# First block's merge: own tile for the sum, gates loaded ahead over blocks, DMA queue in a fixed order, four PSUM banks, squares summed on ScalarE

## The chip, the cores and the metric

The kernel runs on one core of one Trainium2 chip. The metric is the device time of one execution in microseconds; the figure of a kernel is the median of its timed runs. Before the change it is 4016.52 us (three runs, 4011.2 to 4027.01).

## The reference

Two transformer-like blocks on 2048 tokens of 1024 features, all in fp32. The change touches only the end of the first block: two scan results (`o_a`, `o_b`) are normed, gated and projected, mixed by sigmoid gates, projected again, added to the input and layer-normed.

```python
def rms_norm_gated(o, gain, gate):
    o = o * lax.rsqrt(jnp.mean(o * o, axis=-1, keepdims=True) + RMS_EPS) * gain
    return o.reshape(*o.shape[:-2], -1) * jax.nn.silu(gate)

def merge_branches(o_a, o_b, p, a_norm_l, b_norm_l, w_a_out_l, w_b_out_l, w_out_l):
    y_a = rms_norm_gated(o_a, a_norm_l, p['a_gate']) @ w_a_out_l
    y_b = rms_norm_gated(o_b, b_norm_l, p['b_gate']) @ w_b_out_l
    gates = jax.nn.sigmoid(p['merge'].reshape(*p['merge'].shape[:-1], N_BRANCH, D_MODEL))
    return (gates[..., 0, :] * y_a + gates[..., 1, :] * y_b) @ w_out_l
...
        h_lat = layer_norm(DEEPNORM_ALPHA * h_lat + gate_l * sub_lat) * ln_g[l] + ln_b[l]
```

The projections in and the scans come ahead of this; the second block (latent attention and a spatial gating unit) takes `h_lat` as its input.

## The kernel before

Every product of fp32 matrices is three matmuls of a high and a low part (`mm3`, L187 to L189), so each factor has to be split: a cast for the high part on ScalarE (ACT) and a subtraction for the low part on GpSimd (POOL) or VectorE (DVE).

The stage that changes takes the 2048 tokens in eight blocks of 256, in the order 4, 3, 5, 2, 6, 1, 7, 0. A block has three parts:

- `branch`, for each half `j` of 128 tokens: three loads (`d_oa` L1329, `d_ob` L1330, the output gate L1332), SiLU of the gate (L1333), the squares of all eight heads in one ACT instruction (L1335), their sums in one DVE reduction (L1338), the inverse root by small DVE operations (L176 to L184), the scaling (L1340). `turned` then transposes on TensorE (PE) (L1346) and makes `yh`, `yl` (L1351, L1352).
- `merge`, eight steps `m`, one for each 128 output features: load a gate tile `mg` of 128x512 (L1360, three buffers), tanh (L1362), two products `pp` of 12 matmuls each (one for each branch, PSUM tag `pp`, two banks), a multiplication by the gate on DVE after each (L1368), the sum of the two in the place of the first, `mg[:, 0]` (L1370), its high part `mh` on ACT (L1371) and its low part `ml` on POOL (L1372). The buffer of `mg` is thus free when POOL is done.
- `residual`, for each half `j`: load `xt` from the input (L1404, two buffers), 48 products `acc` (six of them for each feature group `k`, which wants `mh` and `ml` of step `k`), scaling and sum (L1412), a layer norm on DVE (L1269 to L1276), the store to `d_h` (L1417). Between the products of the first and the second half PE does the transposes of the next block's branches.

In the last block the branches' place is taken by `ahead_h`: the first weights of the second block are loaded (`raw`, L1303) and split, and rows of `d_h` from earlier blocks are loaded back (L1394) and transposed (`turn`, L1374 on). After the last residual come two more turns, then the second block's first products `d`.

All DMAs of the stage are issued by SyncE (SP), each engine takes its instructions in the order of its own list, and an instruction that waits holds back what stands behind it. PE's order is that of the code (`manual_schedule(engines=PE_ONLY)`); the lists of the other engines, SP's too, are set by a scheduler when the kernel is built. `d_h` is viewed as four rows of the token grid by 32 columns, `xt` and `d_oa` likewise; `d_ob` and the gates have their 128 partitions outermost.

Of the kernel before, what the change touches and what calls it, by code (L numbers as in the profile page):

```python
# [21 lines left out]
P = 128  # L22
D = 1024
KT = 8
# [33 lines left out]
MGB = 3  # L58
# [33 lines left out]
def block_kernel(ctx: ExitStack, tc: tile.TileContext, A, out):  # L92
# [31 lines left out]
    # ---------------------------------------------------------------- constants  # L124
# [6 lines left out]
    def tri(pl, name, base, mult, step, keep=1.0, fill=0.0):  # L131
        """keep where base + mult * partition + step * column >= 0, else fill."""
        t = pl.tile([P, P], F32, name=name)
        pool.memset(t, keep)
        pool.affine_select(out=t, in_=t, pattern=[[step, P]], compare_op=ALU.is_ge, fill=fill, base=base,
                           channel_multiplier=mult)
        return t
# [32 lines left out]
    def rsqrt(pl, v, y, eps, tag, mul=1.0, eng=None):  # L170
        """y = 1 / sqrt(mul * v + eps), by a bit estimate and three Newton steps."""
# [19 lines left out]
    # ---------------------------------------------------------------- u^T: layer norm, modulation  # L191
    # tokens by column of the grid: the first and the second half of the columns, the context
# [64 lines left out]
    def proj_stream(jobs, first=()):  # L257
        """The same for several groups of columns, product by product: yields the time of each."""
# [21 lines left out]
    def ahead_of(groups):  # L280
        """Pieces of several groups of columns, each group's weights loaded before the pieces of the one before."""
# [19 lines left out]
    def rotary(rot, sa, sb, pps):  # L301
        """Rotary tables by token: [cos cos | -sin sin]."""
# [8 lines left out]
        # reduction modulo 2 pi: the quotient in a high and a low part, 2 pi in three  # L311
# [24 lines left out]
    with ExitStack() as s0:  # L336
# [3 lines left out]
        # staging in the place of the second half  # L340
# [33 lines left out]
        with tc.manual_schedule(engines={mybir.EngineType.SP}):  # L374
# [4 lines left out]
            # rows silu(c)^T w_mod of shift and scale, for x and for the context  # L379
# [20 lines left out]
            # and by feature, two blocks of tokens at once  # L400
# [77 lines left out]
        # lower bounds: softmax over the two rows of lb_param, first component  # L478
# [14 lines left out]
        # gate of the residual, silu(c) w + b, as a row: products and sums by partition on VectorE, then over partitions  # L493
# [41 lines left out]
    def interleave(*streams, first=0):  # L535
        """Emit the pieces of several streams evenly mixed; all but the last stream are scheduled ahead of it."""
# [39 lines left out]
    with tc.tile_pool(name="tb", bufs=1, side="right") as tb, tc.tile_pool(name="tbs", bufs=1, space=PSUM) as tbs, \  # L576
# [3 lines left out]
        # 16 columns: the four blocks of 512 tokens side by side in the array  # L580
# [75 lines left out]
        # gate tables of the delta rule  # L656
# [16 lines left out]
        # log1p(e) = 2 atanh(e / (2 + e))  # L673
# [59 lines left out]
    # ---------------------------------------------------------------- delta rule: triangular inverses, attention  # L733
    def pair_mats(h, d, m):
        """Matrices of the pair m of chunks: triangular, attention, scaled queries."""
# [575 lines left out]
    with ExitStack() as mctx:  # L1311
# [111 lines left out]
        for j in range(2):  # L1423
            branch(order[0], j)()
# [628 lines left out]
```

## Time and profile before

| | us |
|---|---|
| median of three runs | 4016.52 |
| profiled execution: its span (no other time of this execution is given) | 4017.7 |
| the changed stage, from the first product of the first block to the last of the last | about 2221 to 2746 |
| first block | 71.5 |
| blocks two to seven, together | 381.2 |
| last block | 72.3 |
| PE busy in the whole span | 3665.3 |
| the first product `d` of the second block | starts at 2758.78 |

A time in the profile is counted from the span's start. A block is taken here to run from the last product `acc` of the block before it to its own last one. A view of waits tells which engine sat idle, and the instruction of another engine, or the DMA, that ended the idle time.

### The profile page before, as it was taken

To read this page: it belongs to the slowest core of one execution; us is meant where nothing else is said; L and a number is where in the kernel's file an instruction comes from. 1 tells how busy PE (TensorE), PEld (TensorE's weight loads), DVE (VectorE), ACT (ScalarE), POOL (GpSimd) and SP (SyncE) were. 2 spreads that over 40 slices of the span, in tenths; PEclk is the share of its full clock that TensorE was granted. 3 is DMA by queue.
4 is the path that set the end of the run, shared out by engine and by line. 5 is a ranking of instruction groups with operands and counts; after the bars stand their busy time and mean duration, and the time that the engine had idled before them with its cause. 6 is when DMAs were issued, how large, how long until landed. Compare 5 with 4: busy or idle time off the path is not lost.

```text
span 4017.7 us, 60424 instructions
## 1 busy us (share of the span) xinstructions
PE 3665.3 (91%) x19974; PEld 2833.5 (71%) x19974; DVE 2421.5 (60%) x6610; ACT 1417.1 (35%) x3703; POOL 1399.3 (35%) x1880
## 2 busy tenths in 40 slices
PE   4799998888999999999889778878999999999999
PEld 0578877777677777777677677777888865555577
DVE  3545658886433333699997746455504377777656
ACT  0544542221133323477665322212212144444400
POOL 2311124431355555354643311111123246666610
PEclk9899999999899999999999889888999999999999
DMA  5322247753354554344444433324433520001254
GB/s 159 110 61 78 87 155 240 222 171 73 112 149 139 151 153 140 109 126 123 132 118 132 145 98 102 103 82 118 128 97 115 171 59 26 26 18 48 63 168 147
DMA packets 515309, 467.44 MB, mean 116 GB/s; under 512 B 87993, under 2 KB 424227, under 8 KB 514804
## 3 DMA queue, kind: packets, MB, share of 16 engines
q1 hardware_dynamic: 514772, 463.53, 38.5%
q8 instruction: 159, 2.61, 0.3%
q14 instruction: 154, 1.26, 0.1%
q0 software_dynamic: 224, 0.05, 0.0%
HBM read 302.08 MB, written 161.37 MB: 115 GB/s over the span
## 4 chain that ended last, share of the span: by engine, by line
PE 32%; DMA 7%; DVE 7%; issue 4%; ACT 1%; SPq 1%; POOL 0%; DVEq 0%; ACTq 0%; POOLq 0%
PE po L1830 3%; PE d L187 3%; PE d L188 3%; PE d L189 3%; DMA d_h<-xt 2%; PE acc L187 2%; PE acc L188 2%; PE acc L189 2%; PE sx L1767 2%; PE st L1797 2%; DMA mg<-d_gate 2%; PE st L1798 1%; PE st L1799 1%; DMA o<-d_ob 1%; DMA raw<-in_w_in_dram 1%
## 5 line engine op out<-in xcount | busy, mean ns | idle before, releaser
L187 PE MATMUL d<-uBh,whi 128*128 128x512 f32 x832 | 363.3, 437 | 17.1 <-ACT gy L835 12.3
L187 PE MATMUL d<-uAh,whi 128*128 128x512 f32 x832 | 361.2, 434 | 8.9 <-DVE gy L845 6.8
L188 PE MATMUL d<-uAl,whi 128*128 128x512 f32 x832 | 336.6, 405 | 6.9 <-DVE uAl L463 6.9
L234 POOL TENSOR_TENSOR wlo<-wraw,whi 128x512 fp32r<-128x512 f32 x128 | 172.8, 1351 | 475.4 <-ACT whi L233 453.4
L188 PE MATMUL d<-uBl,whi 128*128 128x512 f32 x832 | 335.2, 403 | 0.0
L189 PE MATMUL d<-uAh,wlo 128*128 128x512 f32 x832 | 334.0, 402 | 0.0
L189 PE MATMUL d<-uBh,wlo 128*128 128x512 f32 x832 | 332.7, 400 | 0.0
L1803 ACT ACTIVATE pT<-st 128x512 f32<-128x512 f32 (+1 forms) x320 | 170.0, 532 | 234.2 <-PE st L1799 140.5
L1821 POOL TENSOR_TENSOR acc<-acc,pT 128x512 f32<-128x512 f32 (+1 forms) x168 | 186.0, 1107 | 124.8 <-ACT pT L1803 115.0
L1772 DVE TENSOR_REDUCE mx<-sx 128x1 f32<-128x512 f32 (+3 forms) x288 | 169.3, 616 | 50.6 <-PE sx L1767 32.7
L187 PEld LDWEIGHTS d<-uBh,whi 128*128 128x128 f32 x832 | 160.3, 193 | 53.4 <-ACT gy L835 13.1
L1372 POOL TENSOR_TENSOR ml<-mg,mh 128x256 fp32r<-128x256 f32 x64 | 57.7, 903 | 396.9 <-ACT mh L1371 289.0
L187 PEld LDWEIGHTS d<-uAh,whi 128*128 128x128 f32 x832 | 160.9, 193 | 43.5 <-ACT pre L769 5.3
L189 PEld LDWEIGHTS d<-uBh,wlo 128*128 128x128 f32 x832 | 159.8, 192 | 35.7
L189 PEld LDWEIGHTS d<-uAh,wlo 128*128 128x128 f32 x832 | 160.6, 193 | 34.6
L188 PEld LDWEIGHTS d<-uAl,whi 128*128 128x128 f32 x832 | 161.5, 194 | 29.4 <-DVE uAl L463 7.8
L188 PEld LDWEIGHTS d<-uBl,whi 128*128 128x128 f32 x832 | 160.7, 193 | 22.2 <-DVE uBl L463 0.4
L187 PE MATMUL pp<-yh,w_a_out_h 128*128 128x256 f32 x256 | 85.3, 333 | 91.9 <-DVE mg L1368 91.1
L631 DVE SCALAR_TENSOR_TENSOR y<-st,VT,y 128x512 f32<-128x512 f32 (+1 forms) x224 | 164.0, 764 | 4.6
L1830 PE MATMUL po<-pT,v 128*64 128x512 f32 (+3 forms) x640 | 161.3, 563 | 3.3 <-DVE o L1844 3.3
L999 DVE SCALAR_TENSOR_TENSOR r<-pa,c_r,r 128x128 f32<-128x128 f32 x136 | 47.7, 351 | 173.0 <-PE pa L998 169.3
L818 DVE TENSOR_TENSOR Mt<-M 128x1 f32<-128x1 f32 (+40 forms) x155 | 134.8, 870 | 4.0
(596 smaller groups left out, 10585.7 us busy)
## 6 DMA issues: line engine op xcount, KB each, us to landing
wraw<-in_w_in_dram SPq DMA_DIRECT2D x126, 256.0 KB
k<-d_k SPq DMA_DIRECT2D x72, 384.0 KB
d_p<-pre SPq DMA_DIRECT2D x64, 384.0 KB
d_gate<-gy SPq DMA_DIRECT2D x96, 256.0 KB
rows<-d_rows SPq DMA_DIRECT2D x36, 512.0 KB
pr<-d_p SPq DMA_DIRECT2D x64, 256.0 KB
mg<-d_gate SPq DMA_DIRECT2D x64, 256.0 KB
wm<-in_w_mod_dram SPq DMA_DIRECT2D x24, 512.0 KB
```

The costliest lines, as they stand in the source:

```text
L187: pe.matmul(out=out, lhsT=lh, rhs=rh, start=start, stop=False)
L188: pe.matmul(out=out, lhsT=lh, rhs=rl, start=False, stop=False)
L189: pe.matmul(out=out, lhsT=ll, rhs=rh, start=False, stop=stop)
L234: pool.tensor_tensor(out=lo[:, ks, :n], in0=raw[:, :, :n], in1=hi[:, ks, :n].bitcast(F32), op=ALU.subtract)
L631: dve.scalar_tensor_tensor(out=y[:, :w], in0=st[:, o + j:o + j + w], scalar=tap, in1=y[:, :w], op0=ALU.mult, op1=ALU.add)
L818: dve.tensor_tensor(out=t, in0=M[:w, i:i + 1, i + 1:32].to_broadcast([w, L, L]), in1=M[:w, i + 1:32, i + 1:32].rearrange("p j c -> p c j") ...
L1767: pe.matmul(out=ps[:, :w], lhsT=qh[0:96, j * P:(j + 1) * P], rhs=kTh[h % 2][0:96, b * 512:b * 512 + w], start=True, stop=not last)
L1772: dve.tensor_reduce(out=m4[:, j:j + 1] if one else mx[:, j, b:b + 1], in_=ps[:, :w], op=ALU.max, axis=AX.X)
L1797: pe.matmul(out=ps[:, c0:], lhsT=kt_h[0:100, ks], rhs=qh[0:100, c0:], start=True, stop=False)
L1803: act.activation(out=pT[:, c0:], in_=ps[:, c0:], func=AF.Exp, scale=SCALE)
L1821: (dve if on_dve else pool).tensor_tensor(out=acc[:, c0:], in0=src[:, c0:], in1=pT[:, c0:], op=ALU.add)
L1830: pe.matmul(out=po_[h, g][r:r + 64, c0:], lhsT=val[kb][:, vs], rhs=pT_.pop((h, g, kb))[:, c0:], start=kb < 2, stop=kb >= 4 * g + 2, skip_g ...
```

## The change

1. The sum of the two gated products has a tile of its own, `ms` (one buffer); `mh` and `ml` are made from it, and a gate's buffer is free when DVE has added.
2. `MGB` is 4. The gate of step `m + 4`, also of the next block, is loaded after step `m` (`load_gates`, the list `todo`).
3. SP's order is now that of the code (`manual_schedule` for PE and SP): the six branch loads of the next block before the merge, the store of the first half in `residual`, that of the second half in step 1 of the next merge, the loads of `xt` in steps 2 and 5.
4. The products `pp` have a PSUM pool of their own with four banks, which one `turn` uses too.
5. The squares of a head are summed by the ACT instruction that makes them: eight of 128x128 for each half, and no DVE reduction.

```diff
-MGB = 3
+MGB = 4
...
-            sq = br.tile([P, KT, P], F32, tag="sq", name="sq")
-            act.activation(out=sq, in_=o, func=AF.Square)
...
-            dve.tensor_reduce(out=ss, in_=sq, op=ALU.add, axis=AX.X)
+            for k in range(KT):
+                sq = br.tile([P, P], F32, tag="sq", name="sq", bufs=2)
+                act.activation(out=sq, in_=o[:, k, :], func=AF.Square, accum_out=ss[:, k:k + 1])
...
-                    pp = m1s.tile([P, 512], F32, tag="pp", name="pp")[:, 0:256]
+                    pp = m1p.tile([P, 512], F32, tag="pp", name="pp")[:, 0:256]
...
-                dve.tensor_add(mg[:, 0, :], mg[:, 0, :], mg[:, 1, :])
-                act.copy(out=mh[:, m, :], in_=mg[:, 0, :])
-                pool.tensor_tensor(out=ml[:, m, :], in0=mg[:, 0, :], in1=mh[:, m, :].bitcast(F32), op=ALU.subtract)
+                ms = m1.tile([P, 256], F32, tag="ms", name="ms")
+                dve.tensor_add(ms, mg[:, 0, :], mg[:, 1, :])
+                act.copy(out=mh[:, m, :], in_=ms)
+                pool.tensor_tensor(out=ml[:, m, :], in0=ms, in1=mh[:, m, :].bitcast(F32), op=ALU.subtract)
+                for f in also.get(m, ()):
+                    f()
+                if todo:
+                    load_gates(*todo.pop(0))
...
-                sp.dma_start(out=hv[4 * i:4 * i + 4], in_=xt)
+                if j == 0:
+                    store_h(i, xt)
...
+        m1p = mctx.enter_context(tc.tile_pool(name="m1p", bufs=4, space=PSUM))
...
-        mctx.enter_context(tc.manual_schedule(engines=PE_ONLY))
+        mctx.enter_context(tc.manual_schedule(engines={mybir.EngineType.PE, mybir.EngineType.SP}))
+        mgs, xs = [], []
+        todo = [(b, m) for b in order for m in range(KT)]
+        for _ in range(MGB):
+            load_gates(*todo.pop(0))
+        last = None
...
+            also = {1: [], 2: [lambda b=b: load_x(b, 0)], 5: [lambda b=b: load_x(b, 1)]}
+            if last is not None:
+                also[1].append(lambda: store_h(2 * order[n - 1] + 1, last))
+            loaded = [branch_load(order[n + 1], j) for j in range(2)] if n + 1 < len(order) else None
...
+                between = [branch(j, *loaded[j]) for j in range(2)]
...
+            last = done[1][0]
+        store_h(2 * order[-1] + 1, last)
```

**SP, from one block into the next, before.** `o` and `sg` are the branch loads, `mg` the gates, `d_h<-xt` the stores, `xt<-in_x_dram` the loads of the input.

```order
L1332 DMA sg_25829<-d_gate_112 128x8x128
L1329 DMA o_25853<-d_oa_98 128x1x512
L1330 DMA o_25853<-d_ob_99 128x512
L1332 DMA sg_25856<-d_gate_112 128x8x128
L1360 DMA mg_25656<-d_gate_112 128x2x256
L1417 DMA d_h_100<-xt_25362 4x32x1024
L1360 DMA mg_25690<-d_gate_112 128x2x256
L1404 DMA xt_25880<-in_x_dram 128x1x1024
L1360 DMA mg_25724<-d_gate_112 128x2x256
L1360 DMA mg_25758<-d_gate_112 128x2x256
L1417 DMA d_h_100<-xt_25458 4x32x1024
L1360 DMA mg_25792<-d_gate_112 128x2x256
```

The branch loads stand ahead of a block's gates, and each store behind a gate of the next block. The same place now:

```order
L1416 DMA d_h_100<-xt_25220 4x32x1024
L1328 DMA o_25658<-d_oa_98 128x1x512
L1329 DMA o_25658<-d_ob_99 128x512
L1331 DMA sg_25661<-d_gate_112 128x8x128
L1328 DMA o_25663<-d_oa_98 128x1x512
L1329 DMA o_25663<-d_ob_99 128x512
L1331 DMA sg_25666<-d_gate_112 128x8x128
L1361 DMA mg_25701<-d_gate_112 128x2x256
L1416 DMA d_h_100<-xt_25327 4x32x1024
L1361 DMA mg_25737<-d_gate_112 128x2x256
L1412 DMA xt_25772<-in_x_dram 128x1x1024
L1361 DMA mg_25774<-d_gate_112 128x2x256
```

The first half's store now stands ahead of the next branches' loads, and those ahead of the block's first gate (that of step 4); the second half's store stands between the gates of steps 4 and 5.

**ACT, from the last branch of a block into the next merge, before.** `yh` ends a branch; a cast `mh` ends a merge step on ACT.

```order
L1351 CAST yh_24229<-sg_25829 128x4x128 [waits DVE_49] x2
L1335 ACTIVATE sq_26350<-o_26344 128x1024 [waits DMAHW4_49,DMAHW3_49]
L1333 ACTIVATE sg_26347<-sg_26347 128x1024 [waits DMAHW5_49,DVE_49]
L1351 CAST yh_24229<-sg_25856 128x4x128 [waits DVE_49] x2
L1335 ACTIVATE sq_26377<-o_26371 128x1024 [waits DMAHW7_49,DMAHW6_49,Activation_49]
L1333 ACTIVATE sg_26374<-sg_26374 128x1024 [waits DMAHW0_49,DVE_49]
L1371 CAST mh_24418<-mg_26072 128x256 [waits DVE_49,PE_49]
L1371 CAST mh_24418<-mg_26106 128x256 [waits DVE_49,PE_49]
```

Both branches' squares and SiLUs stand ahead of the first cast. The same place now:

```order
L1354 CAST yh_24229<-sg_25666 128x4x128 [waits DVE_49] x2
L1341 ACTIVATE sq_26508,ss_26506<-o_26210 128x128 [waits DMAHW5_49]
L1341 ACTIVATE sq_26510,ss_26506<-o_26210 128x128
L1341 ACTIVATE sq_26512,ss_26506<-o_26210 128x128 [waits Activation_49]
L1341 ACTIVATE sq_26514,ss_26506<-o_26210 128x128 [waits Activation_49]
L1341 ACTIVATE sq_26516,ss_26506<-o_26210 128x128 [waits DMAHW6_49,Activation_49]
L1379 CAST mh_24447<-ms_26249 128x256 [waits DVE_49,PE_49]
L1341 ACTIVATE sq_26518,ss_26506<-o_26210 128x128 [waits Activation_49]
L1341 ACTIVATE sq_26520,ss_26506<-o_26210 128x128 [waits Activation_49]
L1341 ACTIVATE sq_26522,ss_26506<-o_26210 128x128 [waits Activation_49]
L1336 ACTIVATE sg_26213<-sg_26213 128x1024 [waits DMAHW7_49]
L1341 ACTIVATE sq_26543,ss_26541<-o_26215 128x128 [waits DMAHW0_49,Activation_49]
```

Five squares of the next block's first half, which want both of its loads, now stand ahead of the cast of step 0; the rest of the branches is strewn between the casts of steps 0 to 3.

**DVE, in the first steps of a merge, now** (L1375 multiplies by the gate, L1378 adds into `ms`, L1276 ends the layer norm of the block before, whose store follows it).

```order
L1375 SCALAR_TENSOR_TENSOR mg_25916<-mg_25916,pp_26292 128x256 [waits PE_49]
L182 TENSOR_TENSOR ln1rz_26195<-ln1rs_26187 128x1 [waits DVE_49]
L1378 TENSOR_TENSOR ms_26284<-mg_25881 128x256 [waits Pool_49]
L176 TENSOR_SCALAR m1rz_26525<-ss_26506 128x8 [waits Activation_49]
L183 TENSOR_TENSOR ln1rz_26195<-ln1rz_26195,ln1rh_26194 128x1 [waits DVE_49]
L177 TENSOR_SCALAR rs_26507<-m1rz_26525 128x8 [waits DVE_49]
L184 SCALAR_TENSOR_TENSOR ln1rs_26187<-ln1rz_26195,ln1rs_26187 128x1 [waits DVE_49]
L180 TENSOR_SCALAR m1rh_26524<-m1rz_26525 128x8
L178 TENSOR_SCALAR rs_26507<-rs_26507 128x8 [waits DVE_49]
L1276 SCALAR_TENSOR_TENSOR xt_25879<-xt_25879,ln1rs_26187,lnb_24847 128x1024 [waits DVE_49]
L1375 SCALAR_TENSOR_TENSOR mg_25916<-mg_25916,pp_26306 128x256 [waits PE_49]
```

The sum of step 1 waits for POOL (step 0's `ml`), and behind it stand the sums of squares, the end of the layer norm and the second multiplication of step 2. Before, the sum waited for no other engine:

```order
L1370 TENSOR_TENSOR mg_26106<-mg_26106 128x256 [waits DVE_49]
L184 SCALAR_TENSOR_TENSOR rs_26353<-m1rz_26356,rs_26353 128x8 [waits DVE_49]
L178 TENSOR_SCALAR ln1rs_26048<-ln1rs_26048 128x1 [waits DVE_49]
L1340 TENSOR_TENSOR o_26344<-o_26344,rs_26353 128x1024 [waits DMAHW4_49,DMAHW3_49,DVE_49]
L182 TENSOR_TENSOR ln1rz_26056<-ln1rs_26048 128x1 [waits DVE_49]
```

Further on, ACT's list has the tanh of the next block's gates 0 and 1 ahead of this block's casts of steps 5 and 6. On SP, in the last block, all eight loads of the next weights (`raw`, 128x416) now stand ahead of the first loads of `h`; before, two of them did.

## Rows read from the trace of the kernel before

**Rows 1.** Chain of waits, 2100 to 2900 us: shares of the stretch by line.

```profile
by line: issue 17.0%; DMA d_h<-xt 12.4%; DMA mg<-d_gate 8.1%; DMA o<-d_ob 4.3%; PE acc L188 4.3%; PE acc L187 4.3%; PE acc L189 4.1%; DMA raw<-in_w_in_dram 3.6%; PE d L187 2.7%; PE pp L187 2.5%; PE d L188 2.2%; PE d L189 2.2%; PE pp L188 2.
```

**Rows 2.** Windows by block; columns: length, busy time of engines, granted clock, DMA share, GB/s.

```profile
2221.00:2292.50 71.50, 56.08 (x304) 50.18 (x305) 54.12 (x98) 27.97 (x46) 31.08 (x24) 0.85 0.55 160
2292.50:2356.10 63.60, 50.93 (x306) 45.68 (x304) 34.34 (x105) 14.27 (x24) 7.43 (x8) 0.92 0.32 100
...
2611.60:2673.70 62.10, 51.65 (x305) 46.50 (x304) 36.20 (x114) 12.05 (x22) 7.44 (x8) 0.92 0.25 77
2673.70:2746.00 72.30, 54.84 (x321) 49.23 (x319) 29.29 (x73) 14.31 (x30) 14.71 (x17) 0.88 0.36 104
```

**Rows 3.** Groups by line, blocks two to seven: busy, mean ns | idle time before, releaser.

```profile
L187 PE MATMUL pp<-yh,w_a_out_h 128*128 128x256 f32 x192 | 63.3, 329 | 67.1 <-DVE mg L1368 67.1
...
L1372 POOL TENSOR_TENSOR ml<-mg,mh 128x256 fp32r<-128x256 f32 x48 | 44.3, 922 | 343.6 <-ACT mh L1371 264.4 <-issue 49.1 <-PE pp L189 30.1
...
L1362 ACT ACTIVATE mg<-mg 128x512 f32<-128x512 f32 x48 | 30.2, 630 | 198.7 <-DMA mg<-d_gate 197.2 <-POOL ml L1372 1.5
...
L1371 ACT CAST mh<-mg 128x256 fp32r<-128x256 f32 x48 | 19.1, 398 | 33.6 <-DVE rs L184 26.4 <-DVE mg L1370 4.3 <-DVE ln1rs L184 2.8
...
L1276 DVE SCALAR_TENSOR_TENSOR xt<-xt,ln1rs,lnb 128x1024 f32<-128x1024 f32 x13 | 16.6, 1279 | 0.0
...
L1335 ACT ACTIVATE sq<-o 128x1024 f32<-128x1024 f32 x11 | 11.7, 1060 | 25.6 <-DMA o<-d_ob 25.6
```

**Rows 4.** Chain of waits, third and fourth block: start, length, what.

```profile
2366.54 10.06 DMA d_h<-xt
2377.28 10.03 DMA mg<-d_gate
2415.34 5.69 DMA o<-d_ob
2430.55 10.14 DMA d_h<-xt
2441.37 9.30 DMA mg<-d_gate
```

**Rows 5.** Timeline of SP, a merge and the last block: start, time to issue, DMA.

```profile
2440.71 0.57 SPq L1404 DMA_DIRECT2D xt<-in_x_dram  x1
...
2715.02 0.82 SPq L1303 DMA_DIRECT2D raw<-in_w_in_dram  x2
2715.89 2.50 SPq L1394 DMA_DIRECT2D h<-d_h  x4
2719.34 28.02 SPq L1303 DMA_DIRECT2D raw<-in_w_in_dram  x9
```

**Rows 6.** Timeline of ACT: summed squares of an earlier stage; start, length.

```profile
259.29 0.27 ACT L646 ACTIVATE sq<-tr 128x128 f32<-128x128 f32 x1
...
259.53 0.28 ACT L646 ACTIVATE sq<-tr 128x128 f32<-128x128 f32 x1
```

**Rows 7.** Timeline of PE, the last block: start, length modelled, product, idle before.

```profile
2673.51 0.40 PE L189 MATMUL acc<-w_out_h,ml 128*128 128x512 f32 x1
2673.74 0.28 PE L187 MATMUL pp<-yh,w_a_out_h 128*128 128x256 f32 x1
...
2683.69 0.28 PE L189 MATMUL pp<-yh,w_a_out_l 128*128 128x256 f32 x1
...
2695.38 0.58 PE L187 MATMUL pp<-yh,w_a_out_h 128*128 128x256 f32 x1 [9.34 <-DVE mg L1368]
...
2698.96 0.41 PE L188 MATMUL pp<-yl,w_b_out_h 128*128 128x256 f32 x1
```

**Rows 8.** Chain of waits in the last block: one weight piece, then the next.

```profile
2737.90 2.39 DMA raw<-in_w_in_dram
...
2740.93 1.09 POOL lo L1306
2742.03 2.98 DMA raw<-in_w_in_dram
```

More of the change, by code (lines that the diff above doesn't have):

```diff
@@ L1321, in block_kernel, with branch_load @@
         hv = d_h.rearrange("(r w) f -> w r f", w=GW)
-        def branch(b, j):
+        def branch_load(b, j):
             i = 2 * b + j
@@ L1332, in branch @@
             sp.dma_start(out=sg, in_=d_gate[:, 0:8, ts_])
+            return o, sg
+        def branch(j, o, sg):
             act.activation(out=sg, in_=sg, func=AF.Silu)
-            sq = br.tile([P, KT, P], F32, tag="sq", name="sq")
-            act.activation(out=sq, in_=o, func=AF.Square)
             ss = br.tile([P, KT], F32, tag="ss", name="ss", bufs=2)
             rs = br.tile([P, KT], F32, tag="rs", name="rs", bufs=2)
-            dve.tensor_reduce(out=ss, in_=sq, op=ALU.add, axis=AX.X)
+            for k in range(KT):
+                sq = br.tile([P, P], F32, tag="sq", name="sq", bufs=2)
+                act.activation(out=sq, in_=o[:, k, :], func=AF.Square, accum_out=ss[:, k:k + 1])
             rsqrt(br, ss, rs, 1e-6, "m1r", mul=1.0 / P)
@@ L1354, in branch, with load_gates, merge @@
             return turned
-        def merge(b):
+        def load_gates(b, m):
+            mg = m1.tile([P, 2, 256], F32, tag="mg", name="mg", bufs=MGB)
+            sp.dma_start(out=mg, in_=d_gate[:, 8 + m:24:8, b * 256:(b + 1) * 256])
+            mgs.append(mg)
+        def merge(b, also):
             for m in range(KT):
-                bs = slice(b * 256, (b + 1) * 256)
-                mg = m1.tile([P, 2, 256], F32, tag="mg", name="mg", bufs=MGB)
-                sp.dma_start(out=mg, in_=d_gate[:, 8 + m:24:8, bs])
+                mg = mgs.pop(0)
                 act.activation(out=mg, in_=mg, func=AF.Tanh, scale=0.5)
                 for s in range(2):
-                    pp = m1s.tile([P, 512], F32, tag="pp", name="pp")[:, 0:256]
+                    pp = m1p.tile([P, 512], F32, tag="pp", name="pp")[:, 0:256]
                     for k in range(4):
@@ L1377, in turn @@
             for s in range(2):
-                tp = m1s.tile([P, 4, P], F32, tag=tag, name="tp")
+                tp = (m1p if tag == "pp" else m1s).tile([P, 4, P], F32, tag=tag, name="tp")
                 for k in range(4):
@@ L1395, in ahead_h, with load_x, store_h @@
                 turn(t, 8, nw, "(r w)", w0, "tp" if w0 in (16, 8) else "pp")
+        def load_x(b, j):
+            xt = m1.tile([P, D], F32, tag="xt", name="xt", bufs=2)
+            i = 2 * b + j
+            sp.dma_start(out=xt, in_=xv[4 * i:4 * i + 4])
+            xs.append(xt)
+        def store_h(i, xt):
+            sp.dma_start(out=hv[4 * i:4 * i + 4], in_=xt)
         def residual(b, between):
@@ L1402, in residual @@
                 js = slice(j * P, (j + 1) * P)
-                xt = m1.tile([P, D], F32, tag="xt", name="xt", bufs=2)
-                sp.dma_start(out=xt, in_=xv[4 * i:4 * i + 4])
+                xt = xs.pop(0)
                 acc = [m1s.tile([P, 512], F32, tag="acc", name="acc") for s in range(2)]
@@ L1423, in block_kernel @@
         for j in range(2):
-            branch(order[0], j)()
+            branch(j, *branch_load(order[0], j))()
         for _ in left:
@@ L1442, in block_kernel @@
             f()
-        mctx.enter_context(tc.manual_schedule(engines=PE_ONLY))
-        for n, b in enumerate(order):
-            merge(b)
+        mctx.enter_context(tc.manual_schedule(engines={mybir.EngineType.PE, mybir.EngineType.SP}))
[4 more added lines that the diff above has]
+        last = None
+        for n, b in enumerate(order):
+            also = {1: [], 2: [lambda b=b: load_x(b, 0)], 5: [lambda b=b: load_x(b, 1)]}
+            if last is not None:
+                also[1].append(lambda: store_h(2 * order[n - 1] + 1, last))
+            loaded = [branch_load(order[n + 1], j) for j in range(2)] if n + 1 < len(order) else None
+            merge(b, also)
             if n == 0:
@@ L1450, in block_kernel @@
                 lnb = bcast_row(lnp, A["ln_b"][0], D, "lnb")
-            if n + 1 < len(order):
-                between = [branch(order[n + 1], j) for j in range(2)]
+            if loaded:
+                between = [branch(j, *loaded[j]) for j in range(2)]
             else:
```

## The prediction, made before the changed kernel ran

> **What bounds the kernel now.** The windows by block come first [rows 2]. The six middle blocks take 381.2 us, 63.5 each, and PE is busy for about 51.5 of them (first and last of six shown), so some 12 us of each block can be won at most by feeding PE better. The groups by line say where those 12 us lie [rows 3]: the first product of a merge step sat idle for 67.1 us in six blocks, 11.2 a block, released by the DVE multiplication of an earlier step. That is only the nearest link. ACT's tanh was idle for 197.2 us until a gate's DMA landed, and POOL for 264.4 until ACT's cast. So PE waits for a PSUM bank, the bank for DVE, DVE for the tanh, the tanh for a transfer. The chain of waits, read third, names the transfers [rows 1]: 12.4% of 800 us on the stores of `d_h`, 8.1% on gates, 4.3% on `d_ob`.
>
> Why a gate takes so long is in two pairs of rows [rows 4, 5]. A store is issued at 2366.54 and lands 10.06 later; the gate behind it and an `xt` load needs 10.03. A block on, the store needs 10.14, `xt` is issued at 2440.71, and the gate behind that lands 9.30 after its issue at 2441.37. Yet the DMA share of a block is 0.25 to 0.33 [rows 2]. A store or `xt` load (four outer rows) therefore costs ten microseconds of landing time, for itself and for whatever is queued behind it, though most engines are idle. The order of this queue sets the block.
>
> [...]
>
> **Cheap parts.** The tile `ms` and the earlier release of `mg` take POOL's subtraction, 0.92 us, off the gate's reuse [rows 3]; on a queue with ten-microsecond transfers that is nothing. Summing squares on ACT: an earlier stage starts one such 128x128 square every 0.25 us [rows 6], so 8 take 2.0 where one of 1024 took 1.06 [rows 3]; 1.9 us a block more on ACT, which is busy 14 of 64, less on DVE, busy 34 of 64 [rows 2]. By itself nothing; its place in ACT's list is what costs.
>
> **A middle block, rebuilt.** Zero is the block's start, the last product of the block before. A product `pp` takes 0.119 us at full clock (84 from 2673.74 to 2683.69), and `acc` 0.23; after a gap the next 16 steps took 3.58 us, 0.22 each [rows 7], the clock's lower level, so a gap costs about 1.5 more than its length.
>
> First wait. SP's list now has the first half's store at the front, the six branch loads behind it, then gate 4. The store is ready at about 0.2 and lands at 9.9, by 10.06 [rows 4]. `d_oa` is half as many bytes in four rows; between 5.69, the whole landing of a pair today [rows 4], and a quarter of the store's ten, I take 2.8: it lands at 12.7, `d_ob` at 13.4. ACT has five squares ahead of the cast of step 0: cast at 14.1. POOL adds 0.92: 15.3 with the handoffs. On DVE the sum of step 1 waits for that (one `ms`), and behind it stand small operations, the end of the layer norm (1.28) and the second multiplication of step 2: bank free at 17.8. PE meanwhile has the gates of steps 0 to 3 and four banks: nine half steps of 12 products, 9 x 12 x 0.119 = 12.9. It waits 4.9.
>
> Second wait. The layer norm ended on DVE at 17.4, so the second half's store goes out at 17.5 and lands near 29, by 10 to 11. Gate 5 is behind it: 29.9, tanh 0.63, multiplication, bank at 31.0. PE, back at 17.8, has five half steps, 60 products with 16 of them slow: 17.8 + 3.6 + 44 x 0.119 = 26.6, 27.0 with handoffs. It waits 4.0.
>
> Third wait. The load of `xt` for the first half is queued behind that store and lands at 35; the second half's needs the buffer stored at 29 and is issued at 32.5. Behind it stands the next block's gate 1, which lands ten later, 43.2, by the gate's 9.30 and 10.03 [rows 4]. Its tanh stands on ACT ahead of the cast of step 6: cast 44.2, `ml` 45 at the latest. PE is through its products at 35.3 and, after 18 of `acc`, wants `ml` of step 6 at 40; with POOL's part only late by its last piece it goes on at 44.3. It waits 4.3.
>
> From there 78 `acc` products follow, 17.9, with 1.5 for the slow start and about 2 for 16 transposes, 21.4: the block ends at **65.7**. Before it was 63.5. The same kind of sum leaves out handoffs: 51.5 busy and 11.2 of waits give 62.7, 0.8 short. So I take 2.2 + 0.8 = **+3 a block, +18 for six**. The waits themselves are 13.2 against 11.2: the gates do come ahead, but three waits, each behind a four-row transfer, stand where two were. Bounds: if `d_oa` costs nothing behind the store, the first wait is 2.1 and the block 62.9, -0.6; if it costs 5.7 and each gap 2 us more, it is +8.
>
> **First and last block.** The first has no store ahead of its loads and four gates ready; one gate wait less or one more is 8 either way, and I take -2. In the last block the branch loads are gone, so its first wait is too, -5. Against that, the loads of `h` stand behind eight weight loads instead of two. Two buffers turn over every 2742.03 - 2737.90 = 4.13 us for a pair's step [rows 8], about 2 us each, so the six more cost 12.4 before `h` is issued, which today is 0.87 after the first weights [rows 5]. PE's transposes of `h` stand between its `acc` products, in two groups. I take half of the 12.4 as covered by the products ahead of them and the rest as a wait at each group, 6 us twice: +12, an estimate between 0 (all covered) and 20. Sum +7, between 0 and +15. Nothing behind this stage changes place.
>
> **Sum.** 18 - 2 + 7 = +23 us. The profiled span of 4017.7 is 1.2 over the median of 4016.52, so the forecast from the median is **4040 us**.
>
> **Rivals.**
>
> Faster: the gates are really ahead and PE stops waiting for them. Then up to 11.2 a block go, and with half to all of it 34 to 67 less, +5 from the ends: 3957 to 3990, say 3973. For it speaks that gates are issued four steps early and that POOL is out of the loop; against, that the landing times stay and that stores and `xt` now have fixed places ahead of gates. It decides itself by whether the branch loads delay the first cast. [...]
>
> No change: the waits move and the sum stays, 11 to 13 a block. With the +7 of the end and -2 of the start: 4005 to 4028, say 4020. This includes the case that the change doesn't do what it says, because the next block's gates are loaded early but their tanh holds back this block's casts.
>
> Slower by more: one `ms` makes a merge step a chain through three engines, an addition, the cast 0.40, `ml` 0.92 [rows 3] and their handoffs, with squares and SiLU between the casts of steps 0 to 3. A step's 24 products take 2.86 at full clock; if the chain takes over 3.5 in the four steps with branch work, 0.7 x 4 x 8 = 22 more come on top: 4062 to 4090.
>
> **How the numbers follow.** Chances: forecast 0.48 (4021 to 4060), faster 0.19, no change 0.21, slower by more 0.12. A measurement tells about 0.5%, 20 us, from no change: faster means below 3996, slower above 4037. About 0.16 of the forecast's chance lies below 4037, as all of the no-change case does. So faster 0.19, same 0.37, slower 0.44. The range, 3972 to 4066, holds the forecast, no change, and parts of the two others; about 0.1 lies on each side.
>
> **What would show it.** Right: at a block's start the store, then `d_oa`, with ACT's squares idle until about 13 us and PE without a product from 13 to 18; gate 5 landing near 30 behind the second store; a cast of step 6 directly after the tanh of a next gate; PE busy unchanged in a block of 65 to 67. Wrong: merge steps that run through without a gap of 3 us, a store that lands in well under 9 us, or blocks of 57 and less. In the last block, `h` should be issued 12 us or more after the first weights; if PE doesn't wait for it, the +12 is wrong.

## The result, and the profile after

The changed kernel takes 4045.35 us (median of four runs, 4042.35 to 4050.16) against 4015.78 before (four runs, 4011.2 to 4027.01). The ratio is 1.0064, with a 95% interval of 1.0045 to 1.0083: slower by 18 to 33 us. The forecast was 4040. The profiled execution of the changed kernel spans 4040.6 us, 22.9 more than the one before. The medians in the table of the experiments are over all executions of a kernel; one of the ten of e4 took 4098.02 us at a granted clock of 0.87 and is left out of its ratio.

The stretches that answer to [rows 2], first block, blocks two to seven together, last block (columns as there):

```profile
2221.95:2295.87 73.92, 56.91 (x304) 49.19 (x305) 51.89 (x104) 29.00 (x75) 29.50 (x24) 0.82 0.52 150
2295.87:2692.98 397.11, 318.95 (x1825) 283.20 (x1824) 201.25 (x613) 100.61 (x324) 39.16 (x48) 0.89 0.32 96
2692.98:2772.40 79.42, 54.95 (x320) 49.32 (x319) 30.45 (x75) 14.53 (x29) 15.65 (x17) 0.81 0.36 101
```

The six middle blocks take 397.1 us in place of 381.2: 66.2 each against 63.5. That is 15.9 of the 22.9 us. The first block is 2.4 longer. From the last block's start to the first product `d` of the second block it is 88.3 against 85.0 (2692.98 to 2781.29, and 2673.74 to 2758.78), 3.3 more. The rest, 1.3, lies outside these stretches.

The groups by line of blocks two to seven, as in [rows 3], show where the waits went:

```profile
L187 PE MATMUL acc<-w_out_h,mh 128*128 128x512 f32 x192 | 82.2, 428 | 24.6 <-ACT mh L1379 24.6
...
L187 PE MATMUL pp<-yh,w_a_out_h 128*128 128x256 f32 x192 | 59.2, 308 | 15.4 <-DVE mg L1375 15.4
...
L1369 ACT ACTIVATE mg<-mg 128x512 f32<-128x512 f32 x48 | 29.9, 627 | 105.5 <-DMA mg<-d_gate 105.3
L1341 ACT ACTIVATE sq<-o 128x128 f32<-128x128 f32 x96 | 28.5, 298 | 111.0 <-DMA o<-d_oa 111.0
L1378 DVE TENSOR_TENSOR ms<-mg 128x256 f32<-128x256 f32 x48 | 20.3, 422 | 95.2 <-POOL ml L1380 95.2
```

The tanh's wait for gates has fallen from 197.2 to 105.3 us: the gates do come ahead. But the squares now wait 111.0 us for `d_oa`, the sum on DVE waits 95.2 for POOL, which it did not do before, and PE waits 24.6 before `acc`, where the same line of the kernel before (`acc` at L187, blocks two to seven) shows 0.0:

```profile
L187 PE MATMUL acc<-w_out_h,mh 128*128 128x512 f32 x192 | 75.8, 395 | 0.0
```

One block, the fourth, from the product at 2427.33 to that at 2494.69. First its transfers on SP (start, time to issue):

```profile
2427.73 0.55 SPq L1416 DMA_DIRECT2D d_h<-xt  x1
2428.38 0.55 SPq L1328 DMA_DIRECT2D o<-d_oa  x1
...
2445.95 0.54 SPq L1416 DMA_DIRECT2D d_h<-xt  x1
2446.54 0.47 SPq L1361 DMA_DIRECT2D mg<-d_gate  x1
...
2460.78 0.57 SPq L1412 DMA_DIRECT2D xt<-in_x_dram  x1
2465.92 8.79 SPq L1361 DMA_DIRECT2D mg<-d_gate  x3
```

then what ACT makes of them:

```profile
2441.10 0.31 ACT L1341 ACTIVATE sq<-o 128x128 f32<-128x128 f32 x1 [16.30 <-DMA o<-d_oa]
...
2442.58 0.39 ACT L1379 CAST mh<-ms 128x256 fp32r<-128x256 f32 x1
...
2457.98 0.63 ACT L1369 ACTIVATE mg<-mg 128x512 f32<-128x512 f32 x1 [5.29 <-DMA mg<-d_gate]
...
2472.13 0.63 ACT L1369 ACTIVATE mg<-mg 128x512 f32<-128x512 f32 x1 [5.75 <-DMA mg<-d_gate]
2472.67 0.39 ACT L1379 CAST mh<-ms 128x256 fp32r<-128x256 f32 x1
```

DVE's sum of step 1 and the end of the layer norm behind it:

```profile
2443.80 0.43 DVE L1378 TENSOR_TENSOR ms<-mg 128x256 f32<-128x256 f32 x1 [8.36 <-POOL ml L1380]
...
2444.64 1.28 DVE L1276 SCALAR_TENSOR_TENSOR xt<-xt,ln1rs,lnb 128x1024 f32<-128x1024 f32 x1
```

and PE's three waits:

```profile
2446.30 0.58 PE L187 MATMUL pp<-yh,w_b_out_h 128*128 128x256 f32 x1 [5.64 <-DVE mg L1375]
...
2459.12 0.39 PE L187 MATMUL pp<-yh,w_a_out_h 128*128 128x256 f32 x1 [2.33 <-DVE mg L1375]
...
2473.11 0.79 PE L187 MATMUL acc<-w_out_h,mh 128*128 128x512 f32 x1 [4.73 <-ACT mh L1379]
```

The lines form one chain. The store goes out 0.4 us into the block, `d_oa` behind it lands at 13.8, ACT has five squares and then the cast of step 0 at 15.3, POOL lets the sum of step 1 go at 16.5, the layer norm ends, the next store goes out at 18.6 with a gate behind it (tanh at 30.7), and the next block's gate behind the second `xt` (issued at 33.4) has its tanh at 44.8, directly ahead of the cast that `acc` wants. That gate, the first of the three in the last SP line, was issued only at 38.6, when DVE's sum of step 5 had freed its buffer; the chain of waits has it as

```profile
2465.92 6.13 DMA mg<-d_gate
```

### The profile page after: what moved, and what is told of

Same layout as the page of the kernel before. It is cut to its first block, busy times and chain, and to the rows that moved or that the text cites. A ratio compares the mean times of both kernels' runs of the same rounds, so it can differ in the third digit from the quotient of the medians.

```text
span 4040.6 us, 60597 instructions
## 1 busy us (share of the span) xinstructions
PE 3672.8 (91%) x19974; PEld 2837.7 (70%) x19974; DVE 2408.9 (60%) x6594; ACT 1438.0 (36%) x3943; POOL 1392.5 (34%) x1880
## 4 chain that ended last, share of the span: by engine, by line
PE 33%; issue 7%; DVE 6%; DMA 4%; POOL 1%; ACT 1%; SPq 0%; DVEq 0%; POOLq 0%; ACTq 0%
PE d L187 4%; PE d L188 4%; PE d L189 4%; PE po L1863 3%; PE acc L187 2%; PE acc L189 2%; PE acc L188 2%; PE sx L1800 2%; PE st L1830 2%; PE st L1831 1%; PE st L1832 1%; DMA mg<-d_gate 1%; POOL ml L1380 1%; PE ms L187 1%; DMA h<-d_h 1%
## 5 line engine op out<-in xcount | busy, mean ns | idle before, releaser
L187 PE MATMUL d<-uBh,whi 128*128 128x512 f32 x832 | 363.1, 437 | 16.9 <-ACT gy L835 12.5
L187 PE MATMUL d<-uAh,whi 128*128 128x512 f32 x832 | 361.7, 435 | 9.2 <-DVE gy L845 6.7
L187 PEld LDWEIGHTS d<-uBh,whi 128*128 128x128 f32 x832 | 160.3, 193 | 52.9 <-ACT gy L835 13.3
L1380 POOL TENSOR_TENSOR ml<-ms,mh 128x256 fp32r<-128x256 f32 x64 | 51.7, 807 | 416.9 <-ACT mh L1379 416.9
L187 PEld LDWEIGHTS d<-uAh,whi 128*128 128x128 f32 x832 | 160.7, 193 | 43.3 <-ACT pre L769 6.2
L187 PE MATMUL acc<-w_out_h,mh 128*128 128x512 f32 x256 | 109.8, 429 | 31.9 <-ACT mh L1379 31.9
```

Source lines behind the costliest of these rows:

```text
L187: pe.matmul(out=out, lhsT=lh, rhs=rh, start=start, stop=False)
L1380: pool.tensor_tensor(out=ml[:, m, :], in0=ms, in1=mh[:, m, :].bitcast(F32), op=ALU.subtract)
```

## The experiments

The code of `hv`, `xv` and `oav` puts the columns of the token grid outermost, so a whole transfer is four columns of 32 rows; the section on the kernel before has it the other way round. The "four outer rows" are these four columns.

The theory: what costs is the ten microseconds of each transfer with four outer rows, because few of the 16 DMA engines work in it (share 0.27 early in a store's flight) and what is queued behind it lands late (gate 5 above: 11.4 us from its issue at 2446.54 to its tanh); the change moves other work behind such transfers. The rivals: the single tile `ms`, the squares on ACT, the fixed order of SP as such, the loads of `h` in the last block. "Blocks" below is the mean of the six middle blocks, from the first product `pp` of one to that of the next in the trace; each ratio is to runs of the kernel before on the same chip.

| kernel | median us | ratio, 95% interval | blocks us |
|---|---|---|---|
| changed, branch loads late (e1) | 4090.5 | 1.0188, 1.0169 to 1.0207 | 72.5 |
| changed, sum in place (e2) | 4049.4 | 1.0074, 1.0055 to 1.0094 | 67.6 |
| changed, all transfers cut by column (e3) | 3893.9 | 0.9690, 0.9676 to 0.9705 | 46.7 |
| before, all transfers cut by column (e5) | 3914.5 | 0.9739, 0.9724 to 0.9753 | 52.1 |
| changed, h first (e4) | 4026.9 | 1.0014, 1.0002 to 1.0026 | 66.6 |
| changed, cut by features (e6) | 3985.9 | 0.9911, 0.9887 to 0.9936 | 58.7 |
| changed, cut by column and h first (e8) | 3878.4 | 0.9648, 0.9628 to 0.9667 | 46.7 |
| changed, cut by column, two banks (e9) | 3916.0 | 0.9733, 0.9717 to 0.9749 | 49.8 |
| changed, SP scheduled (e7) | 4052.4 | 1.0080, 1.0064 to 1.0096 | 69.7 |
| changed, stores cut by column (e10) | 3973.8 | 0.9883, 0.9865 to 0.9901 | 58.0 |
| before, squares summed on ACT (e11) | 4062.6 | 1.0102, 1.0082 to 1.0122 | 70.1 |
| changed, stores in two DMAs of two columns (e12) | 4110.0 | 1.0223, 1.0205 to 1.0241 | 75.6 |

### The transfers' length: e3, e5, e12, e6, e10

The cut by column, in the changed kernel and in the one before:

```diff
-            sp.dma_start(out=of[:, 0:512], in_=oav[4 * i:4 * i + 4])
+            for q in range(4):
+                sp.dma_start(out=of[32 * q:32 * q + 32, 0:512], in_=oav[4 * i + q])
...
-            sp.dma_start(out=xt, in_=xv[4 * i:4 * i + 4])
+            for q in range(4):
+                sp.dma_start(out=xt[32 * q:32 * q + 32], in_=xv[4 * i + q])
...
-            sp.dma_start(out=hv[4 * i:4 * i + 4], in_=xt)
+            for q in range(4):
+                sp.dma_start(out=hv[4 * i + q], in_=xt[32 * q:32 * q + 32])
```

> The changed kernel with every four-row transfer of the stage (store of d_h, load of xt, load of d_oa) cut into four DMAs of one grid column each, 32 partitions; the order is the same. Theory (a four-row transfer takes ten microseconds because it runs on few DMA engines, and all that is behind it waits): a column's pieces land in 3 to 4 us together, the squares start at 5 to 7 us of a block instead of 13.8, the three waits all but vanish, blocks of 50 to 55 us, time 3945 to 3980. Rival (the landing time is that of the memory or of the store itself, or SP's issuing of 18 more DMAs a block at 0.55 us each takes its place): store still lands after 8 us or more, blocks 64 to 68, time 4035 to 4060.

> The kernel before with the same cut of its stores, xt loads and d_oa loads into four DMAs each, nothing else. If the long transfers are the cause of the 11 us of waits a block there too, its blocks fall from 63.5 to 52 to 57 us and the time to 3950 to 3980. If the kernel before is bound by its gates' late issue (three buffers, freed by POOL), the waits stay above 6 us a block and the time at 3990 to 4010; then the change's gates ahead are worth something once the transfers are short. If the transfers' length is not the cause, 4010 to 4025.

Both landed further out than expected: 3893.9 and 3914.5 us, 119 to 130 us and 99 to 111 us faster than before by the intervals. In the changed kernel PE has no gap left in a middle block. Five of them as one window, and a stretch in which the first store and then `d_oa` are in flight:

```profile
2332.03:2565.63 233.60, 233.37 (x1521) 213.49 (x1520) 171.43 (x511) 84.66 (x270) 33.10 (x40) 1.00 0.48 136
2426.50:2429.50 3.00, 3.00 (x28) 3.00 (x27) 2.92 (x8) 0.00 (x0) 0.00 (x0) 1.00 0.78 208
```

PE is busy 233.4 of 233.6 us at a granted clock of 1.00. The DMA share with store and `d_oa` in flight is 0.78; in the changed kernel it is 0.27 at the same place:

```profile
2429.00:2431.00 2.00, 2.00 (x19) 2.00 (x18) 1.96 (x6) 0.00 (x0) 0.00 (x0) 1.00 0.27 49
```

In e3's chain of waits the last of a store's four pieces lands 3.8 us after its own issue and 5.1 after that of the first, where a whole store took 10.06 and 10.14 [rows 4]:

```profile
2344.23 3.83 DMA d_h<-xt
```

So one cut takes 19.5 us off each block: some 13 of waits and 6.5 of PE's own time (53.2 to 46.7), as the granted clock rises from 0.89 to 1.00. It says that the length of these transfers is the cause of PE's gaps in both kernels. It doesn't yet say that the number of outer rows makes the length; that is what the next two tell.

Two columns to a DMA instead of four, for the stores alone:

```diff
-            sp.dma_start(out=hv[4 * i:4 * i + 4], in_=xt)
+            for q in range(2):
+                sp.dma_start(out=hv[4 * i + 2 * q:4 * i + 2 * q + 2], in_=xt[64 * q:64 * q + 64])
```

> The changed kernel with each store cut in two DMAs of two grid columns, 64 partitions. Each piece is half as large but has two outer rows where the store had four. Theory (the outer rows set the number of DMA engines): a piece runs on two engines, the two pieces on the same two, and the store takes 18 to 22 us to land in place of 10; the waits behind it grow by 8 to 10 us at two places of a block, blocks 74 to 84, time 4095 to 4150. Rival (smaller and more DMAs are faster in any case): blocks 57 to 64, time 3985 to 4030.

The theory's side, 4110.0 us and blocks of 75.6. Two smaller DMAs in place of one make the kernel slower by 65 us against the change. Early in the store's flight, with `d_oa` issued behind it, the share of the 16 DMA engines is 0.13, half of the 0.27 above, and SP and ACT show the delay:

```profile
2442.00:2444.00 2.00, 2.00 (x19) 2.00 (x19) 1.96 (x7) 0.00 (x0) 0.00 (x0) 1.00 0.13 29
```

```profile
2440.56 1.13 SPq L1417 DMA_DIRECT2D d_h<-xt  x2
2441.78 1.68 SPq L1328 DMA_DIRECT2D o<-d_oa  x1
```

```profile
2459.13 0.31 ACT L1341 ACTIVATE sq<-o 128x128 f32<-128x128 f32 x1 [21.50 <-DMA o<-d_oa]
```

`d_oa` lands 18.6 us after the store's issue, against 13.4 in the changed kernel (2427.73 to 2441.10): 5 us more, about half of what was expected, but at the second store too, so that PE's first two waits become 10.8 and 6.2.

Cut by features, four DMAs that keep the four columns outermost:

```diff
-            sp.dma_start(out=hv[4 * i:4 * i + 4], in_=xt)
+            for q in range(4):
+                sp.dma_start(out=hv[4 * i:4 * i + 4, :, 256 * q:256 * q + 256], in_=xt[:, 256 * q:256 * q + 256])
```

The load of `xt` is cut in the same way, that of `d_oa` by 128 features.

> The changed kernel with every four-row transfer cut into four DMAs again, but by features, so that each still has the four grid columns outermost. Theory (the number of outer rows sets how many DMA engines work): nothing is won, the store still takes 9 us or more to land, blocks 65 to 70, time 4035 to 4075. Rival (four DMAs in flight, or shorter ones, are what made the cut by columns fast): blocks below 55, time below 3950.

A miss on both sides: 3985.9 us, blocks of 58.7. With only the store and `d_oa` issued the share is 0.23, and 0.27 early in the store's flight, as with the whole store:

```profile
2463.50:2471.00 7.50, 7.50 (x65) 7.50 (x64) 5.26 (x19) 0.00 (x0) 0.00 (x0) 1.00 0.23 62
2465.00:2468.00 3.00, 3.00 (x27) 3.00 (x26) 2.62 (x9) 0.00 (x0) 0.00 (x0) 1.00 0.27 87
```

```profile
2473.07 0.31 ACT L1342 ACTIVATE sq<-o 128x128 f32<-128x128 f32 x1 [13.06 <-DMA o<-d_oa]
```

The first square starts 10.1 us after the store's issue at 2462.93, not 13.4. It wants only the first quarter of `d_oa` now, and at the same share of 0.27 the store's rows of 1 KB move 87 GB/s where those of 4 KB moved 49 (last columns); how much of the gain is due to which was not separated. By columns the share rises to 0.78, and that is worth 19.5 us a block; by features it stays where it was, and that is worth 7.5. So the larger part comes with the outer rows, and a smaller one with the pieces.

> The changed kernel with the cut by grid column for the two stores of a block alone; the loads of xt and d_oa stay whole. Theory (it is the store ahead of the branch loads and of gate 5 that holds them): the first two waits, 5.6 and 2.4 us, go or shrink to 1 to 2 together, the third stays at 0 to 4; blocks 49 to 57, time 3925 to 3985. Rival (the whole queue of four-row transfers counts, whichever is short): blocks fall by a third of the full cut's 19.5 us only, 59 to 62, time 4000 to 4020.

With the cut of e3 for the stores alone, 3973.8 us, in the theory's band, while the blocks (58.0) lie 1 us above it. In the fourth block PE has 0.4 left of the first wait, 2.2 at step 6, ahead of where the second wait was, and the third at `acc`:

```profile
2431.31 0.39 PE L187 MATMUL pp<-yh,w_a_out_h 128*128 128x256 f32 x1 [2.19 <-DVE mg L1375]
```

```profile
2446.06 0.79 PE L187 MATMUL acc<-w_out_h,mh 128*128 128x512 f32 x1 [3.15 <-ACT mh L1379]
```

The stores are 8 of the 19.5 us, the loads of `xt` and `d_oa` behind and between them the rest.

### Who stands behind them: e1, e2, e7, e11

```diff
-            loaded = [branch_load(order[n + 1], j) for j in range(2)] if n + 1 < len(order) else None
             merge(b, also)
+            loaded = [branch_load(order[n + 1], j) for j in range(2)] if n + 1 < len(order) else None
```

> The changed kernel with one line moved: the six branch loads of the next block stand behind the merge's gates on SP, not ahead of them. Theory (the place of the branch loads behind a store holds ACT's squares, and with them the cast of step 0): the first wait of 5.6 us at 13 us of a block goes, the layer norm and with it the second store come some 7 us earlier, so gate 5 and what is behind it do too; middle blocks fall from 66.2 to 55 to 60 us, in all 3985 to 4010. Rival (one tile ms makes the merge step a chain that is too long): the sums still wait for POOL, blocks stay at 64 to 67 and the time at 4035 to 4050. Rival (the four-row transfers' load alone sets the block, wherever they stand): blocks 63 to 66, 4020 to 4045.

The first wait went, as the theory said, and the time went up to 4090.5, against it and both rivals. PE now waits at the other end of the block, for the transposes that want the branch:

```profile
2490.05 0.55 SPq L1328 DMA_DIRECT2D o<-d_oa  x1
```

```profile
2497.77 0.31 ACT L1341 ACTIVATE sq<-o 128x128 f32<-128x128 f32 x1 [4.83 <-DMA o<-d_oa]
```

```profile
2503.99 0.45 PE L1349 MATMUL tp<-ident,o 128*128 128x128 f32 x1 [6.84 <-DVE o L1343]
```

The block's first product starts at 2452.36; the loads wait in SP's list behind an `xt` load and three gates and are issued at 37.7. The expectation took it for granted that a branch loaded there is still in time. With the first wait gone PE wants its transposes at 44.8 (2503.99 less 6.84), and the squares begin at 45.4. The loads that left the head of the crowded queue met the crowd at its tail.

```diff
-                ms = m1.tile([P, 256], F32, tag="ms", name="ms")
+                ms = mg[:, 0, :]
```

> The changed kernel with the sum put back into the gate's first half: no tile ms, the gate's buffer is free when POOL is done. Theory: the sum of step 1 no longer waits for POOL, so the first wait shrinks by 2 to 4 us, but gate 4 is now issued only after step 0's cast at 15 us and gate 5 still stands behind the second store, so the second wait grows by as much; blocks 65 to 67, time 4035 to 4050. Rival (the single ms is what costs): first wait gone with nothing in its place, blocks 60 to 62, time 4010 to 4020.

4049.4 us, in the theory's band (blocks of 67.6, just above it), but not by its mechanism: PE's first wait is still 5.0 in place of 5.6. Without `ms` DVE sits at the same place for the next instruction in its list, the one that takes the squares' sums, and for the same squares.

```profile
2510.08 0.17 DVE L176 TENSOR_SCALAR m1rz<-ss 128x8 f32<-128x8 f32 x1 [8.39 <-ACT sq L1341]
```

So the single `ms` is where the first wait shows, and not what makes it.

```diff
-        mctx.enter_context(tc.manual_schedule(engines={mybir.EngineType.PE, mybir.EngineType.SP}))
+        mctx.enter_context(tc.manual_schedule(engines=PE_ONLY))
```

> The changed kernel with PE's order alone fixed, so that the scheduler sets SP's list as in the kernel before; ms, four buffers, four banks and summed squares stay. In the list the branch loads stand ahead of the first half's store again, but the xt load and three gates directly behind that store. Theory (the fixed order is what loses): the first wait at 13 us goes, and one of about 4 us stays where gates stand behind the store and an xt load; blocks 57 to 62, time 3985 to 4010. Rival (the single ms or the squares lose it): blocks 65 and more, time above 4035.

The theory's side is wrong: 4052.4, blocks of 69.7, the rival's numbers, though not by the rival's means, as the lists will show. And the cheapest of all parts alone in the kernel before, the eight summed squares:

> The kernel before with the one part that sums the squares on ACT (eight of 128x128 for each half, no DVE reduction), nothing else. The prediction cost this part at nothing by itself: 4008 to 4028. If eight instructions in place of one hold the branch on its way to the transposes, 2.0 us against 1.06 + 1.22 before, it may also gain up to 4 us.

Wrong as well, and by much: 4062.6, slower by 33 to 49 us. ACT's time isn't the reason: it sits idle for 12.6 us before the tanh below. SP's lists are, and they are alike in both. From e11:

```profile
2435.95 0.54 SPq L1417 DMA_DIRECT2D d_h<-xt  x1
2446.37 0.57 SPq L1404 DMA_DIRECT2D xt<-in_x_dram  x1
2447.03 12.15 SPq L1360 DMA_DIRECT2D mg<-d_gate  x3
```

```profile
2455.98 0.63 ACT L1362 ACTIVATE mg<-mg 128x512 f32<-128x512 f32 x1 [12.64 <-DMA mg<-d_gate]
```

and from e7, with PE's wait of that block:

```profile
2444.00 0.54 SPq L1416 DMA_DIRECT2D d_h<-xt  x1
2454.20 0.57 SPq L1412 DMA_DIRECT2D xt<-in_x_dram  x1
2454.86 12.81 SPq L1361 DMA_DIRECT2D mg<-d_gate  x3
```

```profile
2467.68 0.58 PE L187 MATMUL pp<-yh,w_a_out_h 128*128 128x256 f32 x1 [12.42 <-DVE mg L1375]
```

In the kernel before, one gate was issued ahead of that store and one between it and the `xt` load. Where the squares are summed on ACT, the scheduler puts the `xt` load directly behind the store and the gates behind that, and the `xt` load waits for the store's landing because it takes its buffer (it is issued 10.4 us after the store in e11, 10.2 in e7). The first gate behind the store thus lands some twenty microseconds after the store's issue (2435.95 to 2455.98). In a kernel whose lists a scheduler sets, an edit on ACT changed the order of SP. The fixed order of the changed kernel is then a gain of 3.5 us a block against what the scheduler would have done with its other parts (66.2 against 69.7). In the whole kernel little of it is left, 4045.4 against 4052.4 with overlapping intervals: e7's scheduler issues `h` behind two weights, and its way from the last block's start to the first `d` is 74.5 us, not 88.3. Whether the squares would cost nothing with SP's old list wasn't tried. Nor does any run show which part of the change costs the 2.7 us a block: loading the branches late, putting the sum back and freeing SP's order each left the kernel no faster.

### The last block, and the parts that pay: e4, e8, e9

e4 issues the four loads of `h` ahead of the weights:

```diff
...
-                wts = load_w2([(0, 416, 0)])
...
+                for w0, nw in ((16, 16), (32, 16), (8, 8), (48, 16)):
+                    t = box["h1"].tile([P, D], F32, tag="h", name="h")
+                    sp.dma_start(out=t[:8 * nw], in_=d_h.rearrange("(r w) f -> r w f", w=GW)[0:8, w0:w0 + nw])
+                    early.append(t)
+                wts = load_w2([(0, 416, 0)])
```

> The changed kernel with the four loads of h in the last block issued ahead of the eight weight loads. Theory (the end lost its time because h stood behind eight weights): the waits of PE for h, 14.7, 2.0, 3.3 and 1.9 us in the changed kernel, shrink to 0 to 6 in all, middle blocks stay at 66.2, time 4022 to 4034. Rival (h waits for the four-row transfers ahead of it on the same engines, not for the weights): the first wait stays above 9 us, time 4038 to 4050.

4026.9, as expected. In the changed kernel the first load of `h` is issued 17.9 us after the weights, and PE stands before its transposes:

```profile
2720.60 17.89 SPq L1303 DMA_DIRECT2D raw<-in_w_in_dram  x8
2738.54 1.25 SPq L1406 DMA_DIRECT2D h<-d_h  x2
```

```profile
2746.19 1.94 PE L1392 MATMUL tp<-ident,h 128*128 128x128 f32 x8 [14.72 <-DMA h<-d_h]
2750.15 1.94 PE L1392 MATMUL tp<-ident,h 128*128 128x128 f32 x8 [2.01 <-DMA h<-d_h]
```

In e4 these two waits are 2.0 and 2.7, and the way from the last block's start to the first `d` falls from 88.3 to 75.4.

> The changed kernel with both: four-row transfers cut by grid column and h loaded ahead of the weights. With the cut alone the blocks are at 46.6 us with no wait of PE above 1 us, and the last block still waits 10.8 and 2.0 us for h. Theory: these two go, 3876 to 3888. Rival (the weights come later by as much and hold the second block's first products): 3890 to 3900.

3878.4, as expected: faster than the kernel before by 3.5% (3.3 to 3.7). The middle blocks are at PE's own time, and the last stretch falls from 73.4 (e3) to 66.2.

> The changed kernel with the cut by grid column, and two PSUM banks for the branch products in place of four. With short transfers the blocks are 46.6 us with the change and 52.1 without. If the four banks make that difference: blocks 50 to 53, time 3915 to 3935. If the gates ahead and the fixed order do: blocks 46.6 to 48.5, time 3893 to 3908.

The time is in the band of the banks, the blocks just under it: 49.8 us, where four banks give 46.7 and the kernel before, equally cut, 52.1. So with short transfers the change as a whole is worth 5.4 us a block, 3.1 of them by the banks, and 21 us in all (3893.9 against 3914.5). Six blocks make 32; the last stretch, where `h` stands behind eight weights, gives 6.9 back (73.4 against 66.5). With two banks the change gains nothing in all (3916.0 against 3914.5).

## Why the prediction was right, and where it wasn't

The mechanism was right: three waits in a block, each behind a four-row transfer, where there were two. That the span comes out at +22.9 for +23 is luck: the parts are off by -2.1 (the six blocks), +4.4 (the first), -3.7 (the last) and +1.3 (outside the stage).

**The block, rebuilt.** 65.7 by the sum and 66.5 with handoffs; measured 66.2. Event by event, predicted and measured in the fourth block: `d_oa` landed 12.7, 13.8; cast of step 0 14.1, 15.3; first wait over 17.8, 19.0; second store issued 17.5, 18.6; gate 5 there 29.9 and its tanh 30.7; the next block's gate there 43.2 and its tanh 44.8; `acc` goes on 44.3, 45.8. The three waits were 4.9, 4.0 and 4.3; they are 5.6, 3.1 (0.8 before the second product of step 6, then the 2.3 shown) and 4.7. The second is smaller because PE came back 1.2 us late and took 0.5 longer, while the bank came only 0.8 late (31.8 for 31.0). The third came out by another way than foretold: the gate was to be issued directly behind the `xt` load, at about 33, and to need ten; it was issued at 38.6, behind the wait for its buffer, and needed 6.1. That `xt`, issued at 33.4, held it either way is likely, since a gate issued at a DMA share of 0.00, just ahead of a store, had its tanh after 2.9 (kernel before, 2366.09 to 2368.96), but no run separates the two. PE's busy time, 51.7 a block before (310.0 in six), is 53.2: about half of the 2.7 us by which the block grew. It goes with a lower clock after one more gap (granted clock 0.91 and 0.89; 0.50 from 2446 to 2450, behind the first wait), as the step said.

**The six blocks.** +18 predicted, +15.9 measured.

**First block.** -2 predicted, +2.4 measured, inside the 8 given. PE has three waits before `acc` there that it had not before (2.0, 1.2 and 5.4).

**Last block.** +7 predicted, +3.3 measured, with errors that nearly cancel. The delay of `h` was put at 12.4 and is 17.1 (issued 17.9 after the first weights, not 0.87); the wait for it was taken as 12 and is 21.8 (14.7, 2.0, 3.3, 1.9). Half of the delay was counted as covered; none is, since PE also comes to its transposes earlier. The first wait was taken as 5 less; PE's waits for gates in the last merge fell from 13.2 (9.3 and 3.8) to 2.7. And its waits for DVE at the transposes, which the sum left out, fell from 11.8 to 5.8. These three give +5.3, so 2 us of the difference stay unexplained.

**"By itself nothing."** The step on the summed squares failed. It priced ACT's 1.9 us against its slack (a square takes 0.30 us in the changed kernel, eight of them 2.4 and not 2.0) and looked at the list of the final kernel alone. Alone in the kernel before the part costs 33 to 49 us (e11), through SP's list. The prediction didn't need it, since in the changed kernel SP's order is fixed, but the reading "its place in ACT's list is what costs" is only half of it: without that place (e1) the cost moved to the transposes.

**The rivals.** That PE stops waiting for gates came true only with the cut (e3): four banks and gates ahead could not do it while a gate landed behind ten-microsecond transfers. Four PSUM banks in place of two are worth 3.1 us a block in the kernel with short transfers (46.7 against 49.8, e9); with long ones no run has the banks alone. By its own terms (waits of 33.6 to 67.2 less, +5 from the ends) the time of this rival is 3954 to 3988, not 3957 to 3990. The rival of the single `ms` as a chain falls with e2.

**The DMA engines.** The DMA share goes with the outer rows: early in a store's flight it is 0.13 with two (e12), 0.27 with four (the changed kernel) and 0.78 with 32 (e3), of 16 engines 2.1, 4.3 and 12.5. Four DMAs with four outer rows each show 0.27 again (e6). The share is a mean over the 16: the runs don't show which of them worked, nor whether a few worked throughout or more of them in part.

## What to carry to other kernels

Before reordering a DMA queue, look at the DMA share early in a large transfer's flight: if it is as low as here (0.27), cut the transfer so that its outer dimension is larger (32 here, for 4, and a share of 0.78), and only then ask which order and how many buffers are best; here the cut was worth 151 us in the changed kernel, where the change had cost 30, and it turned the change itself into a gain. A change of order can move a wait and not remove it (e1: from 13 us of a block to 44.8), so follow each transfer to what stands behind its consumer on that engine's list. Where a scheduler sets lists, compare the lists of all engines after an edit on one.

## What the runs showed of the hardware that wasn't expected

Behind two DMAs of half the size, with two outer rows each, the next load was there later than behind one with four (18.6 us in place of 13.4 after the store's issue). Four DMAs cut by features, with the same four outer rows and the same DMA share, let the first square start 3.3 us earlier than one whole did; part of that is the smaller first piece of `d_oa`, but rows of 1 KB also moved 87 GB/s at a share of 0.27 where rows of 4 KB moved 49. And with the gaps gone, the middle blocks of e3 repeat to 46.62 us, five of six alike, at a granted clock of 1.00, where the changed kernel has 0.89.
